# Last quarter and two sums of each pair's weights in thirteen small buffers; convolution operands split step by step; merges behind the attention

## The chip, the core and the metric

The kernel runs on one core of one Trainium2 chip. The metric is the device time of one execution in microseconds, from the start of the program to its end; smaller is better. The core has five engines that run side by side, each through its own queue in order: TensorE (PE, with its weight loads as PEld), VectorE (DVE), ScalarE (ACT), GpSimd (POOL) and SyncE (SP), which here only issues DMA transfers. They wait for each other through semaphores.

## What is computed

One decoder block for 1024 tokens of width 1024 in float32. The code below is the reference, cut to its core: one projection gives queries, keys, values, the convolution's input and two gates; dilated attention in three groups of eight heads and a causal depthwise convolution work on them; both results are gated, added and projected; a SwiGLU network follows.

```
h = rms_norm(x, g_pre_mix)
z = h @ w_in
q, k, v, glu_in, z_ga, z_gc = split(z)
# attention: per group g a banded causal softmax with relative bias
alpha = softmax(stack(lses), axis=0)              # over the 3 groups
o = einsum('gbsh,gbshd->bshd', alpha, stack(outs))
y_attn = o @ w_attn_out
# convolution: GLU, 31 taps per channel, layer norm, silu, projection
u = silu(layer_norm(conv(u * sigmoid(gate)) + b_dw))
y_conv = u @ w_conv_out + b_conv_out
merged = sigmoid(z_ga) * y_attn + sigmoid(z_gc) * y_conv
x = x + rms_norm(merged @ w_mix_out, g_post_mix)
h = rms_norm(x, g_pre_ffn)
x = x + rms_norm((silu(gate) * up) @ w_ffn_out, g_post_ffn)
```

## The kernel before

**Products.** Every float32 operand is split into a high and a low half (hi, a copy rounded to the PE's 32-bit format, and lo, the difference), and a product is three matmuls: hi·hi, hi·lo and lo·hi. A "unit" (`unit`, L305 to L309) multiplies one block of 128 weight columns by 512 tokens over eight k-tiles: 24 matmuls. Most of the large projections go through `winograd` (L321 to L323): two blocks of weight columns and all tokens form a 2 x 2 block product that is done with seven products instead of eight. I call this a pair. Its seven products, A11, A12, S2, S1, S3, S4 and A22 in that order, have twelve matmuls each. There are 23 pairs behind the input projection and 20 in the FFN.

**Operands of a pair.** The weights arrive as two rows of blocks, r1 = (a11, a12) and r2 = (a21, a22), each 128x1024. `quarters` prepares the left operands in six pieces, c = 0 to 5, which the loop takes one by one every few k-tiles: c = 0 splits a11 and a12, c = 1 forms the sums S1 and S2 (L215, L216), c = 2 splits these, c = 3 forms S3 and S4 in one 128x1024 slot (L222, L223), c = 4 splits these (`both`: one copy on ACT, L195, and one subtraction, L196), c = 5 splits the last quarter a22 into one slot (copy L231 on ACT, subtraction L232). `wsplit` is the engine of the sums and subtractions: POOL for most of the 23 pairs, DVE in the FFN. In `winograd`, three products add into the bank X; ACT copies it out after A11 (L335) and after S2 (L340), and only then S3 may add to it; L345 copies the bank V of S1.

**Buffers.** Pool "b" has 41 slots of 128x1024 (`slot`), pool "c" has 12 buffers of 128x512 (`half`), pool "d" three slots of 128x1024 (`ring`). A buffer's next writer waits for the last reader of what it held, a matmul, another engine or a store to DRAM.

**Order.** The program is written in one order by hand. `tick` is called after each k-tile of a unit or product; it runs the steps put down for that tick (`later`), takes a piece of a weight split, and moves each background generator (`bg`) on by one step. A generator's `yield n` skips n ticks. So every engine's queue holds its work in the order of the ticks, and an instruction that waits holds up all behind it on its engine. SP issues nearly all DMAs, in order, and each of its DMAs also waits for an earlier one, so that about eight are under way.

**Around attention.** Pairs run from 112 us to 582 us, then the values (L947 to L951), while `conv_norm` normalises the convolution's result: ACT applies silu (L1275) and SP stores each of eight tiles (`d_act`, L1277). Attention runs in the background from about 648 us to 913 us under the values, the late gate and the first conv units: L1050 makes the scores, L1088 transposes, L1095 (ACT) and L1096 (DVE) split the weights, L1123 multiplies them by the values. `conv_split` loads the normalised tiles (`d_act`), 16 halves, and splits each (L1219 on ACT, L1220 on DVE). Sixteen conv units follow the late gate, 0 to 15, two for each of eight weight blocks, ahead of 16 attention output units with half the k-tiles. Before conv unit 0 the code takes all splits of the first token half at once (`while len(B.cop[0]) < 8`). A merge, one for each of four head pairs, loads the three groups' outputs (`d_att`) and weights (`d_w`, in tiles spread over the partitions, two DMAs for each), multiplies and adds them on DVE (L1194, L1198, L1202, L1206, L1209) and splits the sum. It starts when the late gate's operand is released (`hH is None`), so beside the attention's last part. A conv unit's weight split is L188 (ACT) and L189 (DVE), its gate L1547 (DVE).

Of the kernel before, what the change touches and what calls it, by code (L numbers as in the profile page):

```python
# [16 lines left out]
D = 1024  # L17
# [31 lines left out]
NRING = 3  # L49
NHALF = 12  # L50

# [11 lines left out]
class Build:  # L63
# [135 lines left out]
    def quarters(self, i, c):  # L199
# [10 lines left out]
        if c == 0:  # L210
            h, w = self.both(r1)
            o["A11"], o["A12"] = (h[:, l], w[:, l]), (h[:, r], w[:, r])
        elif c == 1:
            self.s12 = self.ring()
            add(self.s12[:, l], a21, a22, op=OP.add)  # L215
            add(self.s12[:, r], self.s12[:, l], a11, op=OP.add)  # L216
        elif c == 2:
            h, w = self.both(self.s12)
            o["S1"], o["S2"] = (h[:, l], w[:, l]), (h[:, r], w[:, r])
        elif c == 3:  # L220
            self.s34 = self.slot()
            add(self.s34[:, l], a11, a21, op=OP.add)  # L222
            add(self.s34[:, r], self.s12[:, r], a12, op=OP.add)  # L223
            self.s12 = None
        elif c == 4:
            h, w = self.both(self.s34)
            o["S3"], o["S4"] = (h[:, l], w[:, l]), (h[:, r], w[:, r])
            self.s34 = None
        else:
            x = self.slot(F32R)  # L230
            nc.scalar.copy(x[:, l], a22)  # L231
            add(x[:, r], a22, f(x[:, l]), op=OP.subtract)  # L232
            o["A22"] = (x[:, l], x[:, r])
            del self.raw[i], self.raw[i - 1], self.hl[i]
# [188 lines left out]
    def consts(self):  # L423
        nc = self.nc
        self.ident = self.small.tile([128, 128], F32, name="ident")
        nc.gpsimd.dma_start(self.ident, self.p_ident)
        tab = self.small.tile([33, 24], F32, name="tab")
        nc.gpsimd.memset(tab[32:33, :], 1.0)
        nc.gpsimd.dma_start(tab[0:32, :], self.p_tab)
        self.tab = tab  # L430
        self.vx = [self.small.tile([128, 66], F32R, name=f"vx{i}") for i in range(4)]
# [15 lines left out]
    def bias_lines(self):  # L447
# [8 lines left out]

        nxt = load(0)
        yield 10
        for g in range(3):
            oh, nxt = nxt, load(g + 1) if g < 2 else None  # L460
            ps = self.bank()
            nc.tensor.matmul(ps[0:8, :384], self.tab[:, g * 8:(g + 1) * 8], oh[0:33, :384],
                             start=True, stop=True)
# [635 lines left out]
    def att_p(self, live, k):  # L1099
# [45 lines left out]
        if u == 6:  # L1145
            nc.sync.dma_start(self.d_att[g, hp], self.O)
            if g == 2:
                self.merges.append(self.bg(self.merge(hp, a["p"][4])))
            self.O = None
# [9 lines left out]
    def merge(self, hp, st):  # L1159

        nc = self.nc
        yield 2
        t = self.tiny(144, "mrg", 2)
        m, r = (t[:, i * 16:(i + 1) * 16].rearrange("p (u e) -> p u e", u=8) for i in range(2))
        w = t[:, 48:96].rearrange("p (g u e) -> p g u e", g=3, u=8)
        low, tot = st[:, :, :, 0:2], st[:, :, :, 2:4]
        nc.vector.tensor_reduce(m, low.rearrange("p g u e -> p u e g"), AX.X, OP.min)
        nc.vector.tensor_tensor(w, low, m.unsqueeze(1).to_broadcast([128, 3, 8, 2]), op=OP.subtract)
        nc.scalar.activation(t[:, 48:96], t[:, 48:96], AF.Exp, scale=-1.0)
        yield 2  # L1170
        nc.vector.tensor_tensor(tot, tot, w, op=OP.mult)
        nc.vector.tensor_reduce(m, tot.rearrange("p g u e -> p u e g"), AX.X, OP.add)
        nc.vector.reciprocal(r, m)
        nc.vector.tensor_tensor(t[:, 96:].rearrange("p (g e u) -> p g u e", g=3, e=2).rearrange("p g u e -> p g u e"), w,
                                r.unsqueeze(1).to_broadcast([128, 3, 8, 2]), op=OP.mult)
        yield 1
        nc.sync.dma_start(self.d_w[hp].rearrange("f (p u) -> p f u", u=8),
                          t[:, 96:].rearrange("p (f u) -> p f u", u=8))
        t = m = r = w = low = tot = None
        yield 6  # L1180

        while self.hH is not None or hp > self.turn:
            yield 0
# [43 lines left out]
    def conv_norm(self):  # L1227
        nc = self.nc
        ones = self.tiny(128, "ones", 1)
        nc.vector.memset(ones, 1.0 / D)  # L1230
        mean = self.slot()
# [9 lines left out]
        for hf in range(2):  # L1241
            s = slice(hf * H, (hf + 1) * H)
            ps = self.bank("s")
            nc.tensor.matmul(ps, ones, self.csum[:, s], start=True, stop=True)
            nc.scalar.copy(mean[:, s], ps)
# [23 lines left out]
        for b in range(9):  # L1269
            if b < 8:  # L1270
                nc.vector.tensor_tensor(A[b], A[b], rs, op=OP.mult)
            if b:
# [3 lines left out]
                                     AF.Silu, bias=self.col(C_BLN + b - 1), scale=self.col(C_GLN + b - 1))  # L1276
                nc.sync.dma_start(self.d_act[b - 1], o)  # L1277
            yield 1
        yield 2
        self.normed = True  # L1280

    def conv_split(self):
# [11 lines left out]
        for i in range(16):  # L1294
            self.cop[i // 8].append(self.split(x.pop(0), H))
            if i < 13:
                x.append(load(i + 3))
            yield 3 if i < 3 else 1
            while i == 3 and self.hH is not None:
                yield 0  # L1300
# [71 lines left out]
def build(ctx, tc, aps):  # L1372
# [81 lines left out]
    def plain_gate(n, job, early):  # L1454
        w = B.weights(job)
        for hf in range(2):
            ps = B.unit(w, B.h_rhs(hf), KT)
            if early:
# [62 lines left out]

    while len(B.cop[0]) < 8:
        next(cs[0])
    mg = {}
# [9 lines left out]
    for n, hf in [(0, 0), (1, 0), (0, 1), (1, 1)] + [(n, hf) for n in range(2, 8) for hf in range(2)]:  # L1534
        if hf == 0:
            ws[n] = B.weights(co[n])
            mg[n] = nxt
            nxt = gate_load(B.d_gc[n + 1]) if n < 7 else (gate_load(B.d_ga[0]), gate_load(B.d_gc[0]))
        while hf == 1 and len(B.cop[1]) < 8:
            next(cs[0])  # L1540
        if B.tags["g"] == 2 and B.fine is None:
            B.banks(g=6, s=2)
        ps = B.unit(ws[n], B.rhs(B.cop[hf]), KT)
        c = mg[n][:, hf * H:(hf + 1) * H]
# [451 lines left out]
```

## Time and profile before

| | us |
|---|---|
| median of three timed runs | 1770.15 (1769.38 to 1771.89) |
| the profiled execution's own time | 1765.19 |
| its span | 1763.3 |
| PE busy in the span | 1711.0 |
| values, convolution and attention's start, from the last pair to the late gate | 582 to 832 |
| late gate and conv units | 832 to 981 |
| attention output units | 981 to 1025 |

The profile is of one execution. Busy times of the engines overlap, and only what holds up the last engine in a chain costs time. In rows of groups, "idle before" is the time in which the engine had nothing to do just before the instructions of the group, with what released it. In rows of the timeline the start comes first, then the duration, and in brackets the idle time before it and what ended it.

### The profile page before, as it was taken

What the parts mean: (1) busy time and instruction counts of PE and PEld (TensorE: products, weight loads), DVE (VectorE), ACT (ScalarE), POOL (GpSimd) and SP (SyncE); (2) the same over time, 40 slices, a digit from 0 to 9 for tenths busy, and PEclk for the clock granted to TensorE, in tenths of its full rate; (3) what the DMA queues carried; (4) which work ended last, traced back from release to release, by engine and by line L of the source; (5) the groups of instructions that cost most, each with busy time, mean ns of one, the idle gap of its engine ahead of it and who ended that gap; (6) DMA issues with size and microseconds to landing.
All of it is one profiled execution on the core that took longest, in us unless ns stands there. A gap on an engine that the chain in (4) does not pass through costs nothing.

```text
span 1763.3 us, 24468 instructions
## 1 busy us (share of the span) xinstructions
PE 1711.0 (97%) x8754; PEld 1441.2 (82%) x8754; DVE 1253.7 (71%) x2215; ACT 787.1 (45%) x1546; POOL 467.2 (26%) x365
## 2 busy tenths in 40 slices
PE   8999999999999999999889999999999999999998
PEld 7788777777777999999678888888888888888786
DVE  6789977777989656777785575585665655667586
ACT  6343343333434476666532246643333333354453
POOL 0017677776777134333310130000000000000000
PEclk9999999999999999999999999999999999999999
DMA  4343433444555968888979742322232232395244
GB/s 161 119 160 99 141 112 121 137 166 146 179 167 136 288 225 230 222 222 216 246 233 312 251 166 97 114 71 91 90 127 106 90 109 106 131 346 167 78 150 150
DMA packets 170870, 285.52 MB, mean 162 GB/s; under 512 B 55505, under 2 KB 86732, under 8 KB 170748
## 3 DMA queue, kind: packets, MB, share of 16 engines
q1 hardware_dynamic: 170348, 283.46, 51.0%
q8 instruction: 69, 1.13, 0.3%
q14 instruction: 53, 0.43, 0.1%
q10 hardware_dynamic: 288, 0.27, 0.0%
q0 software_dynamic: 112, 0.24, 0.0%
HBM read 192.15 MB, written 96.47 MB: 164 GB/s over the span
## 4 chain that ended last, share of the span: by engine, by line
PE 82%; POOL 6%; DMA 5%; ACT 3%; DVE 2%; issue 1%; SPq 0%; DVEq 0%; POOLq 0%; ACTq 0%
PE p L321 14%; PE p L323 14%; PE p L322 14%; PE p L1880 12%; PE p L1609 4%; PE p L305 4%; PE p L309 4%; PE p L307 4%; POOL b L196 3%; PE p L1123 2%; PE p L557 2%; PE p L1050 2%; PE p L949 2%; PE p L947 2%; PE p L951 2%
## 5 line engine op out<-in xcount | busy, mean ns | idle before, releaser
L321 PE MATMUL p<-b,b 128*128 128x512 f32 x1204 | 472.0, 392 | 18.2 <-ACT c L340 18.2
L323 PE MATMUL p<-b,b 128*128 128x512 f32 x1204 | 470.9, 391 | 4.2 <-POOL b L196 4.2
L322 PE MATMUL p<-b,b 128*128 128x512 f32 x1204 | 469.9, 390 | 0.0
L321 PEld LDWEIGHTS p<-b,b 128*128 128x128 f32 x1204 | 226.7, 188 | 72.4 <-ACT c L340 25.2
L323 PEld LDWEIGHTS p<-b,b 128*128 128x128 f32 x1204 | 226.7, 188 | 55.5 <-POOL b L196 8.5
L322 PEld LDWEIGHTS p<-b,b 128*128 128x128 f32 x1204 | 226.8, 188 | 46.7
L1880 PE MATMUL p<-b,b 128*128 128x512 f32 x924 | 210.2, 389 | 0.9 <-ACT b L1219 0.7
L1880 PEld LDWEIGHTS p<-b,b 128*128 128x128 f32 x924 | 173.4, 188 | 37.6 <-ACT b L1219 1.1
L687 DVE SCALAR_TENSOR_TENSOR p<-b,par,p 128x511 f32<-128x511 f32 (+14 forms) x232 | 163.3, 737 | 0.0
L305 PE MATMUL p<-b,b 128*128 128x512 f32 x368 | 147.4, 401 | 0.0
L309 PE MATMUL p<-b,b 128*128 128x512 f32 x368 | 146.5, 398 | 0.6 <-DVE b L189 0.6
L307 PE MATMUL p<-b,b 128*128 128x512 f32 x368 | 146.2, 397 | 0.0
L195 ACT CAST b<-d 128x1024 fp32r<-128x1024 f32 x86 | 90.4, 1052 | 117.1 <-DVE d L216 49.9
L196 POOL TENSOR_TENSOR b<-d,b 128x1024 fp32r<-128x1024 f32 x44 | 105.9, 2406 | 69.6 <-ACT b L195 68.6
L196 DVE TENSOR_TENSOR b<-d,b 128x1024 fp32r<-128x1024 f32 x42 | 51.3, 1221 | 99.7 <-ACT b L195 99.7
L947 PE MATMUL p<-b,b 128*128 128x256 f32 x384 | 112.8, 294 | 0.0
L951 PE MATMUL p<-b,b 128*128 128x256 f32 x384 | 112.2, 292 | 0.0
L949 PE MATMUL p<-b,b 128*128 128x256 f32 x384 | 112.1, 292 | 0.0
L1220 DVE TENSOR_TENSOR b<-c,b 128x512 fp32r<-128x512 f32 x101 | 72.7, 722 | 47.9 <-ACT b L1219 47.8
L1123 PE MATMUL p<-c,b 128*66 128x128 f32 (+1 forms) x620 | 89.2, 243 | 11.2 <-DVE c L1096 5.9
L1219 ACT CAST b<-c 128x512 fp32r<-128x512 f32 x101 | 62.2, 618 | 76.1 <-PE p L1880 24.2
L1220 DVE TENSOR_TENSOR b<-b,b 128x512 fp32r<-128x512 f32 x117 | 80.0, 687 | 18.3 <-ACT b L1219 16.7
(227 smaller groups left out, 3045.7 us busy)
## 6 DMA issues: line engine op xcount, KB each, us to landing
b<-w_in SPq DMA_DIRECT2D x30, 512.0 KB, 4.1
dk<-c SPq DMA_DIRECT2D x48, 256.0 KB, 2.7
dq<-c SPq DMA_DIRECT2D x48, 256.0 KB, 2.6
b<-dq SPq DMA_DIRECT2D x48, 256.0 KB, 5.6
b<-dk SPq DMA_DIRECT2D x48, 256.0 KB, 7.2
b<-w_fi SPq DMA_DIRECT2D x24, 512.0 KB, 4.9
d<-w_in SPq DMA_DIRECT2D x23, 512.0 KB, 3.8
dqS<-c SPq DMA_DIRECT2D x44, 256.0 KB, 2.1
```

What stands on the lines that cost most here:

```text
L196: self.wsplit.tensor_tensor(lo, x, f(hi), op=OP.subtract)
L305: nc.tensor.matmul(ps, hi[:, s], a, start=kt == 0, stop=False)
L307: nc.tensor.matmul(ps, hi[:, s], b, start=False, stop=False)
L309: nc.tensor.matmul(ps, lo[:, s], a, start=False, stop=kt == nk - 1)
L321: nc.tensor.matmul(ps, hi[:, s], a, start=first and kt == 0, stop=False, skip_group_check=True)
L322: nc.tensor.matmul(ps, hi[:, s], b, start=False, stop=False, skip_group_check=True)
L323: nc.tensor.matmul(ps, lo[:, s], a, start=False, stop=kt == 3, skip_group_check=True)
L687: nc.vector.scalar_tensor_tensor(A[i][:, j:], src[i][:, :H - j], w[i], A[i][:, j:], op0=OP.mult, op1=OP.add)
L947: nc.tensor.matmul(o, a, hi[:, s], start=kt == 0, stop=False)
L951: nc.tensor.matmul(o, b, hi[:, s], start=False, stop=kt == KT - 1)
L1220: nc.vector.tensor_tensor(s[:, 512:512 + n], src, f(s[:, :n]), op=OP.subtract)
L1880: nc.tensor.matmul(acc[t], x, y, start=first and e == 0, stop=last and e == 2, skip_group_check=True)
```

## The change

Three things are done.

1. In the pairs, the sums for S3 and S4 go into two small buffers of pool "c" instead of one slot, and each half is copied (L229) and subtracted (L230) by itself into the two slots that hold both hi halves and both lo halves. The last quarter's hi and lo go into two small buffers (L235, L236). Pool "c" has 13 buffers instead of 12, for which the tile `tab` of the bias table, the tile of ones and part of the merges' small tile go.
2. The conv units ask for their operands k-tile by k-tile (`conv_rhs`), and `conv_split` goes on from a flag `room`, set two ticks into the second half of the late gate, with one or two ticks between splits.
3. A merge starts only when the attention has ended (`self.fine is None`); the attention's store of its results is issued one tick later, and `conv_norm` stores its results from ACT's queue.

In the changed kernel the lines shift: L305, L307, L309 become L309, L311, L313; L321 to L323 become L325 to L327; L335, L340 and L345 become L339, L344 and L349; L1050 becomes L1053, L1095 and L1096 become L1098 and L1099, L1123 becomes L1126; L1194, L1198, L1202, L1206 and L1209 become L1197, L1201, L1205, L1209 and L1212; L1219 and L1220 become L1222 and L1223; L1277 becomes L1278, L1547 becomes L1557.

```diff
-NHALF = 12
+NHALF = 13
...
         elif c == 3:
-            self.s34 = self.slot()
-            add(self.s34[:, l], a11, a21, op=OP.add)
-            add(self.s34[:, r], self.s12[:, r], a12, op=OP.add)
+            self.s34 = self.half(), self.half()
+            add(self.s34[0], a11, a21, op=OP.add)
+            add(self.s34[1], self.s12[:, r], a12, op=OP.add)
             self.s12 = None
         elif c == 4:
-            h, w = self.both(self.s34)
-            o["S3"], o["S4"] = (h[:, l], w[:, l]), (h[:, r], w[:, r])
-            self.s34 = None
+            h, w = self.slot(F32R), self.slot(F32R)
+            for n, s in ("S3", l), ("S4", r):
+                x = self.s34[n == "S4"]
+                nc.scalar.copy(h[:, s], x)
+                add(w[:, s], x, f(h[:, s]), op=OP.subtract)
+                o[n] = (h[:, s], w[:, s])
+            self.s34 = x = None
         else:
-            x = self.slot(F32R)
-            nc.scalar.copy(x[:, l], a22)
-            add(x[:, r], a22, f(x[:, l]), op=OP.subtract)
-            o["A22"] = (x[:, l], x[:, r])
+            x, y = self.half(F32R), self.half(F32R)
+            nc.scalar.copy(x, a22)
+            add(y, a22, f(x), op=OP.subtract)
+            o["A22"] = (x, y)
...
-            nc.sync.dma_start(self.d_att[g, hp], self.O)
+            self.later(1, lambda x=self.O: nc.sync.dma_start(self.d_att[g, hp], x))
...
-        while self.hH is not None or hp > self.turn:
+        while self.fine is not None or hp > self.turn:
             yield 0
...
-                nc.sync.dma_start(self.d_act[b - 1], o)
+                nc.scalar.dma_start(self.d_act[b - 1], o)
...
-            yield 3 if i < 3 else 1
-            while i == 3 and self.hH is not None:
+            yield 3 if i < 3 else 1 + i % 2
+            while i == 3 and not self.room:
                 yield 0
...
+            if hf and n == 7 - EARLY:
+
+                B.later(2, lambda: setattr(B, "room", True))
...
-    while len(B.cop[0]) < 8:
-        next(cs[0])
+    def conv_rhs(hf):
+        def at(kt):
+            while len(B.cop[hf]) <= kt:
+                next(cs[0])
+            x = B.cop[hf][kt]
+            return x[:, :H], x[:, H:]
+        return at
+
...
-        while hf == 1 and len(B.cop[1]) < 8:
-            next(cs[0])
...
-        ps = B.unit(ws[n], B.rhs(B.cop[hf]), KT)
+        ps = B.unit(ws[n], conv_rhs(hf), KT)
```

**ACT and POOL in a pair.** The rows below are ACT's queue in the pair that starts at 209.42 us, before: `c` and `b` are buffers of the pools, `p` banks, and numbers are names.

```order
L335 COPY c_1887<-p_1885 128x512
L692 COPY c_1512<-p_1571 128x512
L693 COPY b_1923<-p_1571 128x1
L195 CAST b_1932<-b_1894 128x1024
L231 CAST b_1946<-b_1750 128x512
L340 COPY c_1888<-p_1885 128x512
L774 ACTIVATE c_1887<-c_1887 128x512
L345 COPY c_1889<-p_1961 128x512
```

The same place in the changed kernel:

```order
L339 COPY c_1907<-p_1905 128x512
L695 COPY c_1524<-p_1583 128x512
L696 COPY b_1944<-p_1583 128x1
L229 CAST b_1953<-c_1914 128x512
L229 CAST b_1953<-c_1915 128x512
L235 CAST c_1969<-b_1767 128x512
L344 COPY c_1908<-p_1905 128x512
L777 ACTIVATE c_1907<-c_1907 128x512
L349 COPY c_1909<-p_1985 128x512
```

The copy of S3 and S4 is two rows now, and the last quarter's copy (before L231, now L235) writes a buffer of pool "c"; the copy of bank X (L340, L344) still stands behind it.

POOL in the same pair, before:

```order
L656 TENSOR_TENSOR c_1879<-b_1759 128x512
L222 TENSOR_TENSOR b_1894<-d_1748,b_1750 128x512
L223 TENSOR_TENSOR b_1894<-d_1839,d_1748 128x512
L196 TENSOR_TENSOR b_1933<-b_1894,b_1932 128x1024
L232 TENSOR_TENSOR b_1946<-b_1750,b_1946 128x512
L196 TENSOR_TENSOR b_1989<-d_1901,b_1988 128x1024
```

And in the changed kernel:

```order
L659 TENSOR_TENSOR c_1899<-b_1776 128x512
L222 TENSOR_TENSOR c_1914<-d_1765,b_1767 128x512
L223 TENSOR_TENSOR c_1915<-d_1859,d_1765 128x512
L230 TENSOR_TENSOR b_1954<-c_1914,b_1953 128x512
L230 TENSOR_TENSOR b_1954<-c_1915,b_1953 128x512
L236 TENSOR_TENSOR c_1970<-b_1767,c_1969 128x512
L196 TENSOR_TENSOR b_2013<-d_1922,b_2012 128x1024
```

The sums write buffers of pool "c", and one subtraction of 1024 columns became two of 512; the order of the operations is the same.

**DVE around the last merge.** DVE's queue from the fourth merge's first addition (L1202) to the split of the last conv weight block (the L189 that reads b_9800), before; L1547 is the gate of a conv unit, L196 the split of a merged result:

```order
L1202 TENSOR_TENSOR b_9669<-b_9669,b_9682 128x1024
L1547 SCALAR_TENSOR_TENSOR b_9646<-p_9731,par,b_9646 128x512
L1206 TENSOR_TENSOR b_9747<-b_9747,b_9720 128x1024
L1209 TENSOR_TENSOR b_9669<-b_9669,b_9747 128x1024
L1547 SCALAR_TENSOR_TENSOR b_9646<-p_9771,par,b_9646 128x512
L189 TENSOR_TENSOR b_9809<-b_9727,b_9808 128x512
L196 TENSOR_TENSOR b_9816<-b_9669,b_9815 128x1024
L189 TENSOR_TENSOR b_9809<-b_9727,b_9808 128x512
L1547 SCALAR_TENSOR_TENSOR b_9729<-p_9804,par,b_9729 128x512
L1547 SCALAR_TENSOR_TENSOR b_9729<-p_9840,par,b_9729 128x512
L189 TENSOR_TENSOR b_9882<-b_9800,b_9881 128x512 x2
```

In the changed kernel, from the fourth merge's first multiplication (L1197) on; the last conv weight block is read from b_9863:

```order
L1197 TENSOR_TENSOR b_9876<-b_9876,b_9878 128x1024
L196 TENSOR_TENSOR b_9937<-b_9776,b_9936 128x1024
L1201 TENSOR_TENSOR b_9887<-b_9887,b_9889 128x1024
L1557 SCALAR_TENSOR_TENSOR b_9784<-p_9911,par,b_9784 128x512
L1205 TENSOR_TENSOR b_9876<-b_9876,b_9887 128x1024
L189 TENSOR_TENSOR b_9966<-b_9863,b_9965 128x512 x2
L1557 SCALAR_TENSOR_TENSOR b_9865<-p_9954,par,b_9865 128x512
L1209 TENSOR_TENSOR b_9944<-b_9944,b_9927 128x1024
L1212 TENSOR_TENSOR b_9876<-b_9876,b_9944 128x1024
```

The fourth merge was done two weight blocks before the last one; now its two multiplications and its first addition stand directly ahead of the last block's split. By conv units, the four merges start in units 1, 3, 5 and 7 before and in units 5, 7, 9 and 11 now; the last weight block is split in unit 12 and first used in unit 14.

More of the change, by code (lines that the diff above doesn't have):

```diff
@@ L426, in consts @@
         nc.gpsimd.dma_start(self.ident, self.p_ident)
[L427 to L430, printed above, removed]
         self.vx = [self.small.tile([128, 66], F32R, name=f"vx{i}") for i in range(4)]
@@ L457, in bias_lines @@
         nxt = load(0)
+        tab = self.half()
+        nc.gpsimd.memset(tab[32:33, :24], 1.0)
+        nc.gpsimd.dma_start(tab[0:32, :24], self.p_tab)
         yield 10
@@ L461, in bias_lines @@
             ps = self.bank()
-            nc.tensor.matmul(ps[0:8, :384], self.tab[:, g * 8:(g + 1) * 8], oh[0:33, :384],
+            nc.tensor.matmul(ps[0:8, :384], tab[0:33, g * 8:(g + 1) * 8], oh[0:33, :384],
                              start=True, stop=True)
@@ L1162, in merge @@
         yield 2
-        t = self.tiny(144, "mrg", 2)
+        t = self.tiny(128, "mrg", 1)
         m, r = (t[:, i * 16:(i + 1) * 16].rearrange("p (u e) -> p u e", u=8) for i in range(2))
-        w = t[:, 48:96].rearrange("p (g u e) -> p g u e", g=3, u=8)
+        w = t[:, 32:80].rearrange("p (g u e) -> p g u e", g=3, u=8)
         low, tot = st[:, :, :, 0:2], st[:, :, :, 2:4]
@@ L1168, in merge @@
         nc.vector.tensor_tensor(w, low, m.unsqueeze(1).to_broadcast([128, 3, 8, 2]), op=OP.subtract)
-        nc.scalar.activation(t[:, 48:96], t[:, 48:96], AF.Exp, scale=-1.0)
+        nc.scalar.activation(t[:, 32:80], t[:, 32:80], AF.Exp, scale=-1.0)
         yield 2
@@ L1173, in merge @@
         nc.vector.reciprocal(r, m)
-        nc.vector.tensor_tensor(t[:, 96:].rearrange("p (g e u) -> p g u e", g=3, e=2).rearrange("p g u e -> p g u e"), w,
+        nc.vector.tensor_tensor(t[:, 80:].rearrange("p (g e u) -> p g u e", g=3, e=2).rearrange("p g u e -> p g u e"), w,
                                 r.unsqueeze(1).to_broadcast([128, 3, 8, 2]), op=OP.mult)
@@ L1177, in merge @@
         nc.sync.dma_start(self.d_w[hp].rearrange("f (p u) -> p f u", u=8),
-                          t[:, 96:].rearrange("p (f u) -> p f u", u=8))
+                          t[:, 80:].rearrange("p (f u) -> p f u", u=8))
         t = m = r = w = low = tot = None
         yield 6
-        while self.hH is not None or hp > self.turn:
+        while self.fine is not None or hp > self.turn:
             yield 0
@@ L1228, in conv_norm @@
         nc = self.nc
-        ones = self.tiny(128, "ones", 1)
-        nc.vector.memset(ones, 1.0 / D)
         mean = self.slot()
@@ L1243, in conv_norm @@
             ps = self.bank("s")
-            nc.tensor.matmul(ps, ones, self.csum[:, s], start=True, stop=True)
+            nc.tensor.matmul(ps, self.mean_col.to_broadcast([128, 128]), self.csum[:, s], start=True, stop=True)
             nc.scalar.copy(mean[:, s], ps)
@@ L1280, in conv_norm @@
         self.normed = True
+    room = False
     def conv_split(self):
```

## The prediction

> **What bounds the kernel now.** I read the busy shares, then the costliest groups with what ended their idle time, then the windows stage by stage, and last the timeline inside one stalled pair.
>
> ```profile
> PE 1711.0 (97%) x8754; PEld 1441.2 (82%) x8754; DVE 1253.7 (71%) x2215; ACT 787.1 (45%) x1546; POOL 467.2 (26%) x365
> L321 PE MATMUL p<-b,b 128*128 128x512 f32 x1204 | 472.0, 392 | 18.2 <-ACT c L340 18.2
> L323 PE MATMUL p<-b,b 128*128 128x512 f32 x1204 | 470.9, 391 | 4.2 <-POOL b L196 4.2
> L1123 PE MATMUL p<-c,b 128*66 128x128 f32 (+1 forms) x620 | 89.2, 243 | 11.2 <-DVE c L1096 5.9 <-ACT c L1095 4.6
> ```
>
> TensorE (PE) is busy for 97% of the span, so only its idle time, 1763.3 less 1711.0 or 52 us, and time in which it runs slowly can be won. The groups put 22.4 us of the idle time at the Winograd products (L321, L323) and 11.2 at the attention's second product (L1123). By stage:
>
> ```profile
> 169.13:188.17 19.04, 19.04 (x85) 15.77 (x84) 19.04 (x27) 7.15 (x11) 14.46 (x9) 1.00 0.36 111
> 188.17:544.43 356.26, 333.89 (x1426) 267.50 (x1424) 287.36 (x395) 132.43 (x199) 259.77 (x148) 0.99 0.47 145
> 1182.30:1525.00 342.70, 342.70 (x1513) 283.77 (x1512) 201.80 (x271) 115.86 (x163) 0.00 (x0) 1.00 0.30 104
> ```
>
> Columns: window and length, busy time of PE, PEld, DVE, ACT and POOL with their instructions, granted clock, DMA share, GB/s. The pair at 169.13 has no idle time: 19.04 us for 84 matmuls, 0.2267 each, 2.72 for a product of twelve. The seventeen pairs from 188.17 to 544.43 take 356.26 us where 17 x 19.04 = 323.7 would do: **32.6 us are lost there**. The FFN pairs lose nothing (342.70 busy of 342.70). Inside the pair that starts at 209.42:
>
> ```profile
> 220.38 2.38 POOL L196 TENSOR_TENSOR b<-b,b 128x1024 fp32r<-128x1024 f32 x1 [5.44 <-PE p L322]
> 220.50 0.62 ACT L231 CAST b<-b 128x512 fp32r<-128x512 f32 x1 [4.33 <-PE p L323]
> 221.02 0.58 ACT L340 COPY c<-p 128x512 f32<-128x512 f32 x1
> 221.66 0.50 PE L321 MATMUL p<-b,b 128*128 128x512 f32 x1 [1.19 <-ACT c L340]
> 222.81 0.50 PE L323 MATMUL p<-b,b 128*128 128x512 f32 x1 [0.42 <-POOL b L196]
> ```
>
> Product S3 is due four products after the start, at 209.42 + 4 x 2.72 = 220.30. Two instructions sat until then: the last quarter's copy (L231, ACT idle 4.33) and the low half of S3 and S4 (L196, POOL idle 5.44). Both are released by the end of product S1, whose operands held the 128x1024 slots that they write. Behind L231 in ACT's queue stands L340, the copy of the bank that S3 goes on adding to: first stall, 1.19. S3's low half then takes 2.38: second stall, 0.42.
>
> **The pairs after the change.** The sums for S3 and S4 lie in two small buffers, the last quarter's split in two more. In the order rows ACT has two half copies (L229), L235 and L344 in a row, POOL two L230 and L236. None takes a slot that S1 frees. L229 needs POOL's sums and a slot whose last reader was product A12, which ends 5.44 us into the pair.
>
> ```profile
> 213.64 1.30 POOL L223 TENSOR_TENSOR b<-d,d 128x512 f32<-128x512 f32 x1
> 402.31 1.29 POOL L223 TENSOR_TENSOR b<-d,d 128x512 f32<-128x512 f32 x1
> L232 POOL TENSOR_TENSOR b<-b,b 128x512 fp32r<-128x512 f32 x17 | 24.7, 1454 | 4.4 <-ACT b L231 3.6 <-PE p L322 0.7
> ```
>
> For the pair at 209.42: POOL's second sum ended at 214.94 and A12 ended at 214.86. A half copy takes 0.62 (L231), a half subtraction 1.45 (L232): L229 runs from 215.0 to 216.2, L235 to 216.9, L344 from the end of S2 (217.58) to 218.2. The first L230 ends at 217.1, the second at 218.5, L236 at 220.0. S3 is due at 220.30, S4 at 223.02, A22 at 225.74: nothing is late, and S3's low half has 3 us to spare. The tightest pair that I found starts at 395.51: its second sum ends at 403.60, S3 is due at 406.39, and 403.60 + 0.62 + 1.45 = 405.7 leaves 0.7. POOL pays 2 x 1.45 for 2.38, so 259.77 / 17 = 15.3 us a pair become 15.8 of 19.04; DVE's 287.36 / 17 = 16.9 fit too.
>
> The price is a new cover: these buffers are free only once earlier stores out of them have landed.
>
> ```profile
> dk<-c SPq DMA_DIRECT2D x48, 256.0 KB, 2.7
> dqS<-c SPq DMA_DIRECT2D x44, 256.0 KB, 2.1
> ```
>
> No row of before shows that wait. Below it costs nothing (a store lands in 2.7 us and a buffer comes round after most of a pair); above, a landing of 2.7 us in place of the stall gives the whole 32.6 back. I take 0.6 for it, by the landing row that is far shorter than a pair: **term one, -32**. In the FFN the same edits add a copy and a subtraction per pair to DVE (201.80 of 342.70 busy) and ACT (115.86): nothing.
>
> **The start of attention.** Its first products wait for keys:
>
> ```profile
> 662.44 0.42 PE L1050 MATMUL p<-b,b 128*128 128x128 f32 x2 [1.87 <-DMA b<-dk]
> 663.63 0.43 PE L1050 MATMUL p<-b,b 128*128 128x128 f32 x2 [0.77 <-DMA b<-dk]
> 642.40 3.64 SPq L1277 DMA_DIRECT2D dact<-b  x5
> ```
>
> SP issued the last convolution results at 642.40, with the loads for these keys behind them. The change issues these eight stores from ACT, so SP no longer waits for ACT in between. Bounds: nothing, if the keys' own chain is as late, and 2.64. I take **-2**. Against it: the Trainium skill, "DMA: Bandwidth & Descriptors", section "Issuing engines are not separate DMA queues", says that issuing from several engines saves only the sequencer's time to issue. By that rule the sum would be 2 us smaller; the trace shows SP's queue held up in order, which the rule does not speak of. On ACT the eight issues cost at most 8 x 0.73 (3.64 / 5), beside value products that wait for neither.
>
> **From the end of the late gate to the end of attention (856.6 to 913.5).** Here attention, convolution splits and the first merge and a half lie together.
>
> ```profile
> 856.60:913.50 56.90, 46.26 (x289) 36.67 (x287) 45.82 (x119) 28.45 (x95) 13.60 (x16) 0.91 0.86 242
> 860.00:865.00 5.00, 1.66 (x8) 0.77 (x6) 2.75 (x9) 3.50 (x10) 1.60 (x3) 0.84 1.01 301
> 865.00:870.00 5.00, 4.88 (x19) 4.03 (x20) 3.65 (x9) 2.80 (x11) 4.68 (x6) 0.50 1.04 316
> 875.00:880.00 5.00, 2.78 (x22) 1.99 (x19) 2.96 (x10) 1.93 (x9) 0.00 (x0) 1.00 1.07 277
> 880.00:885.00 5.00, 5.00 (x27) 4.20 (x28) 2.42 (x8) 1.83 (x7) 0.00 (x0) 0.66 1.04 347
> 890.00:895.00 5.00, 2.76 (x19) 2.26 (x20) 4.96 (x11) 3.32 (x13) 3.14 (x3) 1.00 0.75 171
> ```
>
> PE idles 56.90 - 46.26 = 10.6 us, and the clock of 0.91 costs 46.26 x 0.09 = 4.2 more. Until 890 the DMA is full (share above 1) and ACT waits for it with attention's copies behind; at 890 DVE is full (4.96 of 5) with merges and splits between attention's operations. The change takes every merge out of this stretch and spreads the splits. Left are attention and splits, so I leave 3 of the 14.8 us: **-12** (bounds -4, half the idle time and no clock, and -14.8).
>
> The clock falls to 0.50 right after a window with 3.34 us idle, and to 0.66 after one with 2.22. The Trainium skill, "TensorE: Matmul & The Clock Gate", section "HAM oscillation — how this bites in real kernels", sets the bound for such a drop at idle gaps above about 3.4 us. By the letter the second drop, 5.00 x 0.34 = 1.7 us, would not come from idle time and would stay, and the sum be 1.7 smaller; the rows show it behind shorter gaps, so I count it as won.
>
> **What the merges cost afterwards.** Attention ends in the middle of conv unit 3, and all four merges' loads now come after it. Their sizes and the rates:
>
> ```profile
> b<-datt SPq DMA_DIRECT2D x12, 512.0 KB, 8.0
> b<-dw SPq DMA_DIRECT2D x24, 256.0 KB, 9.4
> 917.00:957.00 40.00, 39.36 (x174) 32.28 (x173) 26.39 (x34) 5.55 (x9) 0.00 (x0) 1.00 1.03 326
> 885.00:890.00 5.00, 3.78 (x26) 2.93 (x25) 4.23 (x15) 3.42 (x12) 0.00 (x0) 1.00 1.02 352
> 940.00:950.00 10.00, 9.36 (x42) 7.44 (x41) 7.03 (x7) 2.09 (x3) 0.00 (x0) 1.00 1.04 295
> 945.18 1.23 DVE L1194 TENSOR_TENSOR b<-b,b 128x1024 f32<-128x1024 f32 x1 [1.84 <-DMA b<-dw]
> 948.11 0.69 DVE L189 TENSOR_TENSOR b<-b,b 128x512 fp32r<-128x512 f32 x1
> 948.85 0.50 PE L309 MATMUL p<-b,b 128*128 128x512 f32 x1 [0.64 <-DVE b L189]
> ```
>
> The last three rows show the mechanism at small scale: a merge's multiplication waits for its load on DVE, the weight split L189 is queued behind it, and PE waits 0.64 for that split. After the change the split of the last weight block stands on DVE behind the fourth merge's second multiplication (order rows). Up to that one's load, SP issues 11 of the 12 datt loads, 22 of the 24 dw loads and 13 other transfers of 512 KB: 11 x 0.524 + 22 x 0.262 + 13 x 0.524 = 18.3 MB, at 326 GB/s 56.3 us. With 0.7 until the first issue and 2.1 to land that is 59.1 us after attention; multiplication, gate, addition and split (1.23 + 0.75 + 1.23 + 0.69, less overlap) end at 63. PE reaches unit 14, the first to use that block, after 10.5 units of 24 matmuls, 10.5 x 5.44 = 57.1. So PE waits **+6** at conv units 12 to 14, in place of the 0.64. At 352 GB/s it would be 2, at 295 12. The fourth merge's end, some 3 us on, is in time for the attention output units.
>
> **The sum.** -32 - 2 - 12 + 6 = **-40** on the profiled execution's 1765.2 us (span 1763.3), so 1725. That run lies 5 us under the median of the timed runs, 1770.15; from the median it is 1730, which I predict.
>
> **Rivals.** (a) The late merges cost nothing or 12 us: 1724 or 1736. For the first speaks that DMA reached 352 GB/s, for the second 295 with merge loads. (b) The pairs keep half their loss, because a small buffer's store is late or POOL is (0.7 us to spare in one pair): 1746. Against: nothing that PE then waits for is released by S1. (c) The small buffers or DVE's longer chain hit the FFN, which is free of idle time now and has DVE do every sum: L222, L223, two L230 and the copies, about 4 us in a row, must end before S3. From the point where DVE reaches them more than 4 us late each of some 20 pairs waits; at 2.2 us, a store's landing, that is +44: 1774, **slower than before**. Against: DVE is busy 59% there. (d) The change does not free the slots as it says, since some other tile still ties L344 to S1's end; then only the rest remains, -8: 1762.
>
> **How the numbers follow.** Forecast 0.56, with 1724 to 1737; merges free 0.12 and dear 0.12; (b) 0.13; (c) 0.03; (d) 0.04. The range 1720 to 1747 leaves out (c), (d) and the edge of (b). A measurement of this kernel tells about 0.2% (3.5 us) from no change. Faster 0.95, same 0.02, slower 0.03.
>
> **What would show it.** The pairs from 188 on at 19.04 us each, no row L321 <- ACT L344 or L323 <- POOL L230; ACT's L229 ending before S2. PE's idle time in the 57 us up to attention's end down to 3 and the clock near 1. A wait of 2 to 12 us for L189 late in the conv units, with DVE waiting for dw or datt ahead of it. Wrong would be: idle time at L222 or L349 for a store, or any idle time in the FFN pairs.

## The result, and the profile after

| | before | changed |
|---|---|---|
| median of the timed runs, us | 1770.34 | 1731.91 (1727.06 to 1733.54) |
| ratio, 95% interval | | 0.9778 (0.9756 to 0.9799) |
| profiled execution, us | 1765.19 | 1730.98 |
| its span, us | 1763.3 | 1729.2 |

The changed kernel is faster by 2.2%. The prediction was 1730. In the two profiled executions, on which everything below rests, the difference is 34.2 us; between the medians it is 38.4, because the profiled execution of before lies 5 us under its median.

First the rows of the changed kernel's page and of its group view that answer to those of before:

```profile
PE 1698.1 (98%) x8754; PEld 1441.0 (83%) x8754; DVE 1255.7 (73%) x2235; ACT 793.6 (46%) x1589; POOL 466.9 (27%) x387
L325 PE MATMUL p<-b,b 128*128 128x512 f32 x1032 | 401.6, 389 | 0.0
L327 PE MATMUL p<-b,b 128*128 128x512 f32 x1032 | 401.5, 389 | 0.0
L313 PE MATMUL p<-b,b 128*128 128x512 f32 x368 | 147.1, 400 | 9.1 <-DVE b L189 9.1
```

Both stalls of the pairs are gone: L325 and L327 (L321 and L323 before) have no idle time ahead of them. A new entry stands in their place, 9.1 us at the plain units (L313), which wait for DVE's weight splits. The windows of the changed kernel, with the columns of the prediction, are the seventeen pairs, the start of attention, the stretch from conv unit 0 to attention's end, and from there to the attention output units:

```profile
188.17:512.00 323.83, 323.83 (x1431) 268.13 (x1430) 286.61 (x397) 136.14 (x216) 260.64 (x166) 1.00 0.51 160
606.00:632.00 26.00, 21.22 (x165) 20.58 (x164) 16.14 (x46) 21.36 (x47) 8.62 (x11) 0.93 1.02 328
825.30:866.70 41.40, 39.73 (x288) 32.94 (x287) 37.06 (x111) 27.27 (x94) 12.41 (x16) 1.00 0.61 195
866.70:946.70 80.00, 70.89 (x299) 57.44 (x298) 45.96 (x56) 14.13 (x23) 0.74 (x1) 0.96 0.98 303
```

PE is busy for every microsecond of the pairs, and for 39.73 of 41.40 beside attention, where before it was 46.26 of 56.90. Afterwards it idles for 9.1 us at a mean clock of 0.96. At the start of attention it idles for 4.8 of 26 us, and the clock is 0.93.

The stages can be cut at the same instruction in both traces, by the start of the first matmul of each. That gives the bill:

| stage | before | changed | difference | predicted |
|---|---|---|---|---|
| pairs from 188 us on (17) | 357.2 | 323.7 | -33.5 | -32 |
| last pair's end to the late gate | 248.7 | 250.9 | +2.3 | -2 |
| conv unit 0 to conv unit 4, just behind attention's end | 58.3 | 43.1 | -15.3 | -12 |
| conv unit 4 to the attention output units | 66.3 | 78.3 | +12.0 | +6 |
| everything else | 1032.9 | 1033.2 | +0.4 | 0 |

Two terms came out better than forecast, by 1.5 and 3.3 us, and two worse, by 4.3 and 6.0. By the traces the sum is -34.1 where -40 was forecast.

In the pair that starts at 207.13, the timelines of ACT and POOL show why nothing waits any more:

```profile
212.62 1.14 ACT L229 CAST b<-c 128x512 fp32r<-128x512 f32 x2 [1.33 <-PE p L326]
213.66 0.62 ACT L235 CAST c<-b 128x512 fp32r<-128x512 f32 x1
215.49 0.59 ACT L344 COPY c<-p 128x512 f32<-128x512 f32 x1 [1.21 <-PE p L327]
213.32 2.56 POOL L230 TENSOR_TENSOR b<-c,b 128x512 fp32r<-128x512 f32 x2 [0.41 <-ACT b L229]
```

The half copies start 5.5 us into the pair, at the end of A12, as worked out. Bank X is copied at 215.49, right after S2, and both low halves are done at 215.88. S3 is due at 218.01.

### The profile page after: what moved, and what is told of

Same layout as the page of the kernel before. It is cut to its first block, busy times and chain, and to the rows that moved or that the text cites. A ratio compares the mean times of both kernels' runs of the same rounds, so it can differ in the third digit from the quotient of the medians.

```text
span 1729.2 us, 24623 instructions
## 1 busy us (share of the span) xinstructions
PE 1698.1 (98%) x8754; PEld 1441.0 (83%) x8754; DVE 1255.7 (73%) x2235; ACT 793.6 (46%) x1589; POOL 466.9 (27%) x387
## 4 chain that ended last, share of the span: by engine, by line
PE 89%; DMA 5%; ACT 2%; DVE 2%; issue 1%; SPq 1%; POOL 0%; ACTq 0%; DVEq 0%; POOLq 0%
PE p L326 16%; PE p L325 16%; PE p L327 16%; PE p L1890 12%; PE p L1619 4%; PE p L309 3%; PE p L311 3%; PE p L313 3%; PE p L1126 3%; PE p L1053 2%; PE p L950 2%; PE p L952 2%; PE p L954 2%; PE p L560 2%; DMA b<-dw 2%; PE p L1091 2%
## 5 line engine op out<-in xcount | busy, mean ns | idle before, releaser
L325 PE MATMUL p<-b,b 128*128 128x512 f32 x1032 | 401.6, 389 | 0.0
L327 PE MATMUL p<-b,b 128*128 128x512 f32 x1032 | 401.5, 389 | 0.0
L326 PE MATMUL p<-b,b 128*128 128x512 f32 x1032 | 401.5, 389 | 0.0
L325 PEld LDWEIGHTS p<-b,b 128*128 128x128 f32 x1032 | 193.7, 188 | 41.1 <-ACT c L339 0.6
L327 PEld LDWEIGHTS p<-b,b 128*128 128x128 f32 x1032 | 193.7, 188 | 40.1
L326 PEld LDWEIGHTS p<-b,b 128*128 128x128 f32 x1032 | 193.7, 188 | 40.1
L1890 PE MATMUL p<-b,b 128*128 128x512 f32 x924 | 210.2, 389 | 0.9 <-ACT b L1222 0.7
L1890 PEld LDWEIGHTS p<-b,b 128*128 128x128 f32 x924 | 173.4, 188 | 37.6 <-ACT b L1222 1.1
L313 PE MATMUL p<-b,b 128*128 128x512 f32 x368 | 147.1, 400 | 9.1 <-DVE b L189 9.1
L309 PE MATMUL p<-b,b 128*128 128x512 f32 x368 | 147.5, 401 | 0.0
L311 PE MATMUL p<-b,b 128*128 128x512 f32 x368 | 146.6, 398 | 0.0
L196 POOL TENSOR_TENSOR b<-d,b 128x1024 fp32r<-128x1024 f32 x44 | 106.9, 2429 | 101.6 <-ACT b L195 88.5
L196 DVE TENSOR_TENSOR b<-d,b 128x1024 fp32r<-128x1024 f32 x42 | 51.3, 1221 | 105.1 <-ACT b L195 105.1
L1223 DVE TENSOR_TENSOR b<-c,b 128x512 fp32r<-128x512 f32 x101 | 70.9, 702 | 41.6 <-ACT b L1222 40.8
L1222 ACT CAST b<-c 128x512 fp32r<-128x512 f32 x101 | 62.5, 618 | 67.2 <-PE p L1890 22.5
L1223 DVE TENSOR_TENSOR b<-b,b 128x512 fp32r<-128x512 f32 x117 | 79.9, 687 | 18.3 <-ACT b L1222 16.6
L1066 ACT ACTIVATE c<-c,stat 128x128 f32<-128x128 f32 (+1 forms) x192 | 84.9, 445 | 12.3 <-DVE stat L1056 11.6
```

The lines of the kernel that those rows point to most:

```text
L196: self.wsplit.tensor_tensor(lo, x, f(hi), op=OP.subtract)
L309: nc.tensor.matmul(ps, hi[:, s], a, start=kt == 0, stop=False)
L311: nc.tensor.matmul(ps, hi[:, s], b, start=False, stop=False)
L313: nc.tensor.matmul(ps, lo[:, s], a, start=False, stop=kt == nk - 1)
L325: nc.tensor.matmul(ps, hi[:, s], a, start=first and kt == 0, stop=False, skip_group_check=True)
L326: nc.tensor.matmul(ps, hi[:, s], b, start=False, stop=False, skip_group_check=True)
```

## The experiments

The runs below are kernels built from the changed one by the edit shown, unless the text says otherwise. Times are medians of whole runs; of before, 1767.7 to 1771.4 beside each set.

**Each part of the pair change by itself.** First the last quarter goes back into one large slot:

```diff
-            x, y = self.half(F32R), self.half(F32R)
-            nc.scalar.copy(x, a22)
-            add(y, a22, f(x), op=OP.subtract)
-            o["A22"] = (x, y)
+            x = self.slot(F32R)
+            nc.scalar.copy(x[:, l], a22)
+            add(x[:, r], a22, f(x[:, l]), op=OP.subtract)
+            o["A22"] = (x[:, l], x[:, r])
```

> The changed kernel with the last quarter's split back in one large slot; the two sums stay in small buffers. Theory A (two separate waits on slots that S1 frees): in 11 of the 17 pairs the quarter's copy waits for S1 again with the copy of bank X behind it, 1.36 us each as the pair at 209 shows in the kernel before, 15 us in all; no wait for the low half of S3. Rival B (only the two sums in one large slot mattered): no more idle time than in the changed kernel.

It took 1748.6 us (two runs), and the seventeen pairs 14.3 us more than without idle time. In the pair that starts at 208.3 the timeline reads:

```profile
219.22 0.62 ACT L235 CAST b<-b 128x512 fp32r<-128x512 f32 x1 [4.26 <-issue]
219.74 0.58 ACT L344 COPY c<-p 128x512 f32<-128x512 f32 x1
220.37 0.50 PE L325 MATMUL p<-b,b 128*128 128x512 f32 x1 [1.01 <-ACT c L344]
```

ACT sits until S1 has ended and PE waits for the copy of bank X behind it. The profile names no releaser here; that the wait ends with S1 is seen from the time. There is no wait for POOL. Then the two sums go back into one slot, with one split of 1024 columns, and the quarter stays in small buffers:

```diff
-            self.s34 = self.half(), self.half()
+            self.s34 = self.slot()
...
-            for n, s in ("S3", l), ("S4", r):
...
+            h, w = self.both(self.s34)
+            o["S3"], o["S4"] = (h[:, l], w[:, l]), (h[:, r], w[:, r])
```

> The changed kernel with the sums for S3 and S4 back in one slot and one split of 1024 columns; the last quarter stays in small buffers. Theory A: in 11 or 12 of the 17 pairs POOL's L196 starts only when S1 ends and takes 2.4 us, the third matmul of S3 waits for it: 2.2 us each as in the pairs at 481 to 544 before, 24 to 26 us in all; no wait for the copy of bank X. Rival B (only the last quarter's slot mattered, the second stall followed from the first): less than 5 us. With theory A the two parts are not additive: 15 and 25 against 33 for both.

It took 1761.3 us (1761.1 to 1769.4), the pairs 24.5 us too many, in eleven of them:

```profile
220.42 2.37 POOL L196 TENSOR_TENSOR b<-b,b 128x1024 fp32r<-128x1024 f32 x1 [5.56 <-PE p L322]
222.84 0.50 PE L323 MATMUL p<-b,b 128*128 128x512 f32 x1 [1.89 <-POOL b L196]
```

Theory A holds in both: 14.3 us against 15, and 24.5 against 24 to 26. The two waits overlap in time: 14.3 and 24.5 us alone, 33.5 together. So by these runs the quarter's edit without the other would have won 9.0 us and the sums' edit without the other 19.2; the last 5.3 needed both.

**The thirteenth buffer.** One constant each, 12 and 11 small buffers, one run each.

```diff
-NHALF = 13
+NHALF = 12
```

> The changed kernel with 12 small buffers, as many as before the change. Theory A (a store lands in under 4 us and a buffer comes round after most of a pair): the pairs stay at 19.04 us, at most 1 us of idle time in all of them; the thirteenth buffer costs and brings nothing. Rival B (the thirteenth buffer is what keeps stores out of the way): waits at L222, L344 or L349 for a store, 5 us or more in the 17 pairs.

> The changed kernel with 11 small buffers. Theory A: the cover thins, a buffer comes round half a pair after its store was issued; up to 3 us of idle time in the pairs. Rival B: each pair waits for a store, 17 x 1 us or more.

They took 1733.0 and 1739.6 us. Neither has idle time in the pairs; these are the windows of the pairs, with 12 and then with 11 buffers, and of the stretch beside attention with 11:

```profile
188.20:512.00 323.80, 323.80 (x1430) 268.12 (x1429) 286.45 (x397) 136.65 (x217) 260.75 (x165) 1.00 0.50 160
188.20:512.00 323.80, 323.80 (x1430) 268.10 (x1430) 284.54 (x397) 136.53 (x217) 261.54 (x165) 1.00 0.50 160
828.00:875.60 47.60, 43.53 (x294) 35.80 (x293) 38.92 (x113) 28.18 (x95) 12.16 (x16) 0.96 0.58 177
```

The stores out of the small buffers never hold up the pairs. With 12 nothing measurable is lost; with 11 it is attention, which shares the buffers: ACT's writes into them (L1098) wait 6.1 us for products that still read them (L1126), which they do not do in the changed kernel. PE idles for 4.1 us in this stretch, 3.0 of it in one wait for keys; why these come late is not shown. The thirteenth brings nothing that these runs show.

**The stores at the start of attention.** SP issues the eight stores again.

```diff
-                nc.scalar.dma_start(self.d_act[b - 1], o)
+                nc.sync.dma_start(self.d_act[b - 1], o)
```

> The changed kernel with one thing undone: the eight stores of the normalised convolution results are issued by SP again, not by ACT. Theory A (ACT's queue pays for the issues: each holds ACT about 0.33 us and lets it idle 0.4 before, so the copies of the value banks and the weight split behind them come late): the PE waits for L965 (2.4 us) and for L1056 (2.4 us) at 607 to 620 go, the stage from the last pair to the late gate shrinks by 3 to 5 us, the whole kernel by as much. Rival B (the stage is longer because the pairs before it no longer stall, so DVE and ACT come to it with more left to do): the waits stay within 1 us and the time with them. If the keys are late again as in the kernel before, a wait of up to 2.6 us for dk returns and the gain is 1 to 2 us.

1734.2 us (1731.1 to 1738.0), no gain. The waits of PE, with their total, count and longest, in the changed kernel and then in this one:

```profile
PE p L950 <- ACT d L965: 2.4, 2, 1.5
PE p L1053 <- DVE stat L1056: 2.4, 1, 2.4
PE p L1053 <- DMA b<-dk: 1.3, 1, 1.3
```

```profile
PE p L1053 <- DMA b<-dk: 3.6, 3, 1.6
PE p L1053 <- DVE stat L1056: 2.3, 1, 2.3
```

Theory A is half right: ACT's issues do make L965 late, and those 2.4 us go. But 2.2 us of waiting for keys come back at 631 and 633 us, as in the kernel before, and the wait for L1056 stays. (The other 1.4 us for keys, like the 1.3 in the changed kernel, stand near 840, beside attention.) The wait moves from one queue to the other. That DVE is late at L1056 fits rival B in part: its chain of the convolution's normalisation (L1272) starts 50.6 us after the last pair's end here, 49.0 before. A second delay, by way of ACT, is shown under "The start of attention" below.

**Merges beside attention, and the splits.** First only the merges' condition goes back:

```diff
-        while self.fine is not None or hp > self.turn:
+        while self.hH is not None or hp > self.turn:
```

> The changed kernel with one thing undone: a merge may start when the late gate's operand is released, beside the last part of attention, as before; the step by step splits stay. Theory A (the merges made the idle time beside attention): 7 to 13 of the 15 us gained between 857 and 913 are lost again, the wait for the weight splits late in the conv units (9.1 us, with the slower clock behind it 12) goes, and the whole is within 4 us of the changed kernel. Rival B (the burst of four forced splits made it): the stretch beside attention keeps nearly all of its gain and the wait for the splits goes too, so this kernel is 9 to 12 us faster than the changed one.

1730.1 us (1729.8 to 1733.0), as fast as the changed kernel. The two stretches of the same windows:

```profile
825.60:881.60 56.00, 47.20 (x296) 38.59 (x295) 43.44 (x118) 28.33 (x95) 12.79 (x16) 0.88 0.90 250
881.60:948.70 67.10, 65.56 (x289) 53.96 (x288) 38.21 (x50) 13.24 (x23) 0.74 (x1) 1.00 0.90 296
```

12.8 of the 15.3 us beside attention are lost again, and 11.1 of the 12.0 behind it come back: theory A. The move of the merges, taken alone, was worth 1.7 us in the trace, which is no more than these runs can tell. Then the merges stay behind attention, and the forced splits and their old spacing come back:

```diff
-            yield 3 if i < 3 else 1 + i % 2
-            while i == 3 and not self.room:
+            yield 3 if i < 3 else 1
+            while i == 3 and self.hH is not None:
...
+    while len(B.cop[0]) < 8:
+        next(cs[0])
```

> The changed kernel with the four forced splits ahead of conv unit 0 and the old spacing; merges stay behind attention. Theory A (the merges' transfers made most of the idle time beside attention): 2 to 5 us of the 15 us gained there are lost, with the first wait for L1098 or L1099 near the start of conv unit 0; the waits for L189 late in the conv units stay. Rival B (the burst alone stalls attention): 8 us or more are lost.

1735.7 us (two runs); the stretch beside attention grows by 5.5 us, a little over theory A's range and short of B's. So merges and burst each cause idle time, and overlap: 12.8 and 5.5 against 15.3. What joins them is one wait of ACT, in the view of waits for this stretch: before, in the changed kernel, with early merges, with the burst.

```profile
ACT b L1219 <- DMA c<-dact: 11.9, 5, 3.2
```

```profile
ACT b L1222 <- DMA c<-dact: 0.7, 1, 0.7
```

```profile
ACT b L1222 <- DMA c<-dact: 8.2, 2, 5.2
```

```profile
ACT b L1222 <- DMA c<-dact: 2.9, 1, 2.9
```

ACT's copy of a convolution operand waits for its load, and attention's copies stand behind it.

**Loading the merges' tiles ahead.** The waits for L189 come from transfers that pile up once attention has ended. Two kernels load a part of them beside attention, without any arithmetic of the merges there: the first merge's two pairs of tiles, and then each merge's one merge ahead.

```diff
-        while self.fine is not None or hp > self.turn:
+        while self.hH is not None or hp > self.turn:
             yield 0
...
         yield 8
+        while self.fine is not None or hp > self.turn:
+            yield 0
```

> The changed kernel, but the first merge's first two pairs of tiles (2.1 MB) are loaded beside attention, from conv unit 0 on; each merge's arithmetic still waits for attention's end. Theory A (the stall of 9.1 us late in the conv units is the transfers' backlog after attention, and DMA had room beside attention): 2.1 MB at 310 GB/s are 6.8 us less backlog, the waits for L189 shrink to 2 to 5 us, attention keeps its gain, the whole is 5 to 9 us faster than the changed kernel, 1722 to 1727. Rival B (these loads come ahead of attention's own loads and make the idle time that the merges made before): the stretch from 825 to 867 grows by 3 to 8 us and nothing is won.

> As the last kernel, with the loads of each merge one merge ahead: 4.2 MB beside attention, and every merge's first two pairs loaded some two conv units earlier; the DVE operations stand at the same places in the order as in the changed kernel. Theory A: no wait for L189 over 1.5 us is left, the clock stays at 1 behind it, 10 to 13 us faster than the changed kernel, about 1720. Rival B: attention's stretch grows by 5 to 10 us and eats it.

The second differs by `hp > self.turn + 1` in the first condition and a `yield 10` behind the second. They took 1744.6 (1742.4 to 1747.9) and 1737.4 us (1736.8 to 1738.3): both slower than the changed kernel. In the second no wait for L189 is left, as theory A had it, but the stretch from conv unit 0 to conv unit 4 takes 62.9 us instead of 43.1, and the timeline of ACT shows rival B at work:

```profile
848.42 0.62 ACT L1225 CAST b<-c 128x512 fp32r<-128x512 f32 x1 [7.56 <-DMA c<-dact]
862.06 0.62 ACT L1225 CAST b<-c 128x512 fp32r<-128x512 f32 x1 [9.04 <-DMA c<-dact]
```

My premise was wrong: DMA's mean rate beside attention, 195 GB/s, looked like room, but cut finer the changed kernel's windows are full and then empty:

```profile
835.00:845.00 10.00, 8.71 (x64) 7.28 (x64) 9.38 (x27) 7.13 (x26) 1.64 (x3) 1.00 1.05 337
850.00:855.00 5.00, 4.77 (x35) 3.94 (x34) 4.80 (x19) 2.20 (x11) 0.36 (x1) 1.00 0.11 42
860.00:867.00 7.00, 7.00 (x50) 5.56 (x50) 5.41 (x14) 1.64 (x4) 0.00 (x0) 1.00 0.06 6
```

The first of the two also gained nothing later: there the waits for L189 even grew to 12.8 us. Its merges come earlier in DVE's order, which the second's do not, so it mixes two causes, and I draw nothing more from it.

So the next kernel is the second of these, with the loads held until the operands' loads have all been asked for:

```diff
-        while self.hH is not None or hp > self.turn + 1:
+        while len(self.cop[1]) < 5 or hp > self.turn + 1:
```

> As the kernel with each merge's loads one merge ahead, but the first loads wait until the last convolution operand has been asked for (conv unit 15.5 of the old count, some 2 units before attention's end). The windows of the changed kernel show the DMA full until 845 and nearly idle from 850 to 867 (share 0.06 to 0.17), room for some 5.5 MB. Theory A (what counts is where the transfers lie: beside the operands' loads they stall attention, after it they pile up): attention keeps its 41 us, no wait for L189 over 1.5 us, 9 to 12 us faster than the changed kernel, 1719 to 1723. Rival B (any early merge load disturbs attention): attention's stretch grows by over 3 us.

**1717.75 us** (1716.41 to 1718.77), ratio to before 0.971 (0.9694 to 0.9727), against 0.9778 (0.9756 to 0.9799) for the changed kernel: some 12 us faster than that, and faster than both. The windows from 850 to attention's end, and from there to the attention output units:

```profile
850.00:867.00 17.00, 16.70 (x118) 13.47 (x118) 15.33 (x44) 8.18 (x30) 1.09 (x2) 1.00 1.04 274
867.40:934.50 67.10, 67.10 (x300) 55.54 (x299) 45.68 (x56) 14.06 (x23) 0.74 (x1) 1.00 0.95 294
```

DMA fills the gap, attention keeps its pace, and PE does not idle once in the 67 us behind it. Last, the same with the eight stores issued by POOL (`nc.gpsimd.dma_start`):

> The same, and the eight stores of the normalised convolution results issued by POOL. Theory A (neither ACT nor SP is then held up at the start of attention): the waits for L965 (2.4 us) go and those for dk do not come back beyond 1 us, 2 to 3 us faster than the last kernel. Rival B (POOL prepares attention's keys and queries and is held up by the stores, which wait for ACT): waits for POOL or dk of 2 us or more and nothing won. The wait for L1056 (2.4 us) stays in both.

1717.5 us (1715.7 to 1721.5), the same. The waits for L965 went, and against the expectation the one for L1056 too, but at the start of attention PE now waits 2.6 us for POOL (L888, L889). The stage from the last pair to the late gate is 1.2 us shorter (248.8 against 250.1), and the stretch beside attention 1.4 longer, with a wait of 2.5 us for keys at 838, where the kernel with the stores on ACT waits 1.8. Three queues were tried for these stores, and each left a wait in front of attention, POOL the shortest.

## Why the prediction came out, step by step

**The pairs: right.** Mechanism, places and times inside the pair are as worked out, and the size is 33.5 against 32. No wait for a store in a small buffer was seen, so the 0.6 kept for it was not needed. The window in the prediction ends at 544.43, inside the seventeenth pair, which ends at 545.33: the loss was 33.5 us and not 32.6, and all of it went. The rivals of half the loss staying, of trouble in the FFN (no idle time in it) and of slots that stay tied did not occur.

**The start of attention: wrong.** The step that failed reads "I take -2"; it was +2.3. Its gain came as foreseen: the waits for keys, 2.6 us before, are gone from this stage. What failed is the price: I costed ACT's eight issues as lying beside value products "that wait for neither", but the values' own copies out of their banks (L965) stand in ACT's queue behind them, and PE waits 2.4 us for those banks. ACT's part of a weight split (L188) stands there too. DVE's part (L189) waits for it, and L1056 is behind that on DVE:

```profile
617.88 0.62 ACT L188 CAST b<-b 128x512 fp32r<-128x512 f32 x1 [0.40 <-ACT b L1276]
618.53 0.69 DVE L189 TENSOR_TENSOR b<-b,b 128x512 fp32r<-128x512 f32 x1 [6.59 <-ACT b L188]
```

This L188 starts 68.0 us after the last pair's end here and 63.3 before. In the last two kernels it is 67.4 with the stores on ACT, with the wait for L1056, and 63.4 with the stores on POOL, without it. With the stores on SP it is 65.2, held up 1.2 us by its own load. So the wait for L1056, 2.4 us where it was 0.5, hangs on ACT's queue as well. Last, the granted clock was 0.50 from 621.0 to 624.4, behind these waits; that costs 1.7 us, and the kernel before has full clock through this whole stage. The run with the stores back on SP shows that the waits for L965 are due to ACT's issues; it has the low clock too.

The Trainium skill, "DMA: Bandwidth & Descriptors", section "Issuing engines are not separate DMA queues", says that starting DMAs from several engines saves only the time to start them. Over the whole stage nothing was saved here.

**Beside attention: right, too cautious.** 15.3 instead of 12; PE's idle time went from 10.6 to 1.7 us, and the clock is back at 1.00. (The bound of -4, called half the idle time, should have read -5.3.) The cause named was merges' loads and DVE together. The runs show that transfers ahead of the operands' loads are enough, since a kernel with the loads but without any merge arithmetic there lost even more; what DVE adds was not separated.

**The give-back: right mechanism, half the size.** The term "+6" measured 12.0 net. The rows are of the kind foreseen: DVE waits for dw with the split behind it, and PE waits for the split. But the prediction had all of the wait behind the fourth merge, and it came in three parts: 0.7 us in conv unit 10, 4.76 in unit 12 behind the third merge, and only 3.65 in unit 14 behind the fourth.

```profile
915.80 1.22 DVE L1201 TENSOR_TENSOR b<-b,b 128x1024 f32<-128x1024 f32 x1 [4.21 <-DMA b<-dw]
917.60 0.68 DVE L189 TENSOR_TENSOR b<-b,b 128x512 fp32r<-128x512 f32 x1
918.34 0.80 PE L313 MATMUL p<-b,b 128*128 128x512 f32 x1 [4.76 <-DVE b L189]
918.34:923.00 4.66, 4.66 (x14) 3.79 (x15) 4.58 (x5) 0.00 (x0) 0.00 (x0) 0.68 1.04 364
930.88 1.23 DVE L1201 TENSOR_TENSOR b<-b,b 128x1024 f32<-128x1024 f32 x1 [0.87 <-DMA b<-dw]
934.55 0.50 PE L313 MATMUL p<-b,b 128*128 128x512 f32 x1 [3.65 <-DVE b L189]
```

Two things were mis-sized. The rate was 303 GB/s over the stretch and not 326, so 18.3 MB take 60.4 us and not 56.3: 4 us more, and most of the way from 6 to the 9.1 us of idle time. And each of the two long waits was followed by a slow clock that the sum left out: 0.68 for the 4.66 us after the first long one, 0.69 after the second, some 3 us together. I had counted that effect as a gain beside attention and then forgot it as a cost. Moving the merges was therefore nearly neutral. The stretches beside and behind attention together gained 3.3 us, for which the spread splits are needed (with the burst put back the two take 6.0 us more); the start of attention took 2.3 back. The change's gain is the pairs' 33.5 us.

The Trainium skill's bound of about 3.4 us of idle time for a clock drop ("TensorE: Matmul & The Clock Gate", "HAM oscillation — how this bites in real kernels") agrees with these two drops, after 4.76 and 3.65 us. It does not agree with the third in the same trace, at 621.0, where the longest wait was 2.4 us. The drop in the kernel before whose longest gap was 1.77 us went with the gap, as the rows had it.

**Total and range.** 1731.9 lies 2 us from the forecast, and part of that is luck. By the profiled executions the change was worth 34 us and not 40, and even there two terms that were 4.8 us too cautious cover part of two that were 10.3 us too hopeful. The medians differ by 4 us more, which lie within the scatter of the kernel before.

## What to carry to other kernels

A pool's buffer is part of the order: where a copy writes a slot that a product still reads, all that stands behind it on its engine waits for that product, and smaller buffers with an earlier last reader take the wait away. Work that is moved out of a crowded stretch takes its transfers along; look at the DMA share in windows as short as the gaps in question, both where the loads leave and where they go, and put the loads into the gap and the arithmetic behind it. When a wait can go to one of three queues, ask what stands behind it in each before choosing.

## What had not been expected of the hardware

Single waits of PE of 4.76 and 3.65 us cost more than their length: the granted clock was 0.68 and 0.69 in the about 5 us behind each and the first matmul after the longer one took 0.80 us in place of 0.39. Shorter waits can do the same. Most waits of 1.2 us between products in the kernel before did not, and the pair at 209 runs at 1.00, but two of its pairs have a drop, behind 1.81 us of idle time and behind 1.19 and 0.42 us close together. The first is in this window:

```profile
395.51:418.29 22.78, 20.97 (x85) 16.82 (x84) 17.60 (x24) 8.86 (x13) 17.11 (x10) 0.93 0.52 165
```

Cut finer, the clock of the thirteen traces is always 1.00 or 0.50, and the changes lie on a grid of 3.41 us. Leaving out the first 20 and the last 25 us, every fall to 0.50 follows a step of this grid in which PE idled for 1.62 us or more, so about half of it; of the steps with 1.63 to 1.77 us four were not followed by one, and every step with more was. With 12 small buffers the same wait of 2.37 us ahead of attention's first products lies across two steps, 1.2 us in each, and the clock stays at 1.00 there. So in these traces it is the idle time within one step that goes with the drop, and not the length of a single wait.
